# Gate, pool-output and attention-output projections with tokens on partitions, and four k-groups in place of five

## The chip, the core and the metric

The kernel runs on one core of a Trainium2 chip. The metric is the device time of one execution in microseconds (us), the median of repeated runs. The core has four engines that matter here: TensorE (PE in the profile, with its weight loads as PEld), VectorE (DVE), ScalarE (ACT) and GpSimd (POOL). SP is the queue that issues the loads.

## The reference

One decoder layer over 256 tokens and 2048 features, in float32, with an input projection 9280 columns wide:

```python
h = layer_norm(x) * (1.0 + scale) + shift          # shift, scale, gate = silu(c) @ w_ada + b_ada
q_lat, kv_lat, mla_gate, pool_in, pool_gate, gate_logits = split(h @ w_in)
y_mla = mla_mixer(q_lat, kv_lat, ...)               # 16 heads, causal
y_mla = (y_mla * silu(mla_gate)) @ w_mla_o
y_pool = pool_mixer(pool_in, w_pool_g, pool_scale)  # causal means over 2, 4, 8, 16 tokens, then w_pool_g
y_pool = (y_pool * silu(pool_gate)) @ w_pool_o
g_mla, g_pool = split(sigmoid(gate_logits + b_gates))
y = (g_mla * y_mla + g_pool * y_pool) @ w_out
out = layer_norm(alpha * x + (1.0 + gate) * y, ln_g, ln_b)
```

## The kernel before

Every float32 operand of a large product is split into two float32r tiles, `hi` and `lo`, whose sum is the operand. A product is then three matmuls: `mm3` (lines 95 to 98) multiplies high by high, high by low and low by high, with the weights standing still in the array (128 features) and all 256 tokens streaming. So the results of `w_in`, `w_pool_o` and `w_mla_o` have features on partitions. The last projection (`out_mm`, lines 922 to 928) is the other way round: 128 tokens stand still and 512 columns of weights stream.

Weights come in blocks of up to 1 MB into one of 5 raw tiles (`Raw`, `RAWB`), and are taken from there in parts of up to 1024 columns (`Job`): ScalarE writes `hi` (line 92), VectorE writes `lo` (line 93), into one of 4 pairs (`HB`). `execute` lets the loads and the splits run ahead of the matmuls as far as these tiles reach.

The work is a list of jobs, put in order by `weave`, which sets side work at given fractions of the main work:

1. The input projection goes over its 16 k-tiles in five groups (`KGROUPS`: 2, 3, 3, 4, 4 k-tiles). In each group all 72 feature tiles are done; `win_jobs` adds the group's sum to a tile in SBUF, by ScalarE in the first group (line 430) and by VectorE in the others (line 432). After the last group `post` applies silu or sigmoid.
2. Into each group but the last, the modulation of the next group's k-tiles is woven (`ada_jobs`): `w_ada` is multiplied by silu(c) and summed on VectorE (line 275), and `finish` sums over partitions on TensorE (line 300) and makes the next `hh` and `hl`. This is woven into the first 0.80 to 0.85 of a group (`WB`).
3. Into the last group go the norm of the latents, the rotary key, the pooling means and their mixing (`mix_jobs`).
4. Attention by pairs of heads, with the projections of the next pair and `pool_out` woven in. A head is done in four steps: `scores`, `normal` (scales the probabilities on VectorE), `transp` (three transposes on TensorE), `values` (features on partitions).
5. `mla_out`, which also merges the branches into `mh` and `ml`; then the output projection, the residual and the closing norm. The gate's modulation (`gate_jobs`) is woven into stages 4 and 5.

A scheduler sets each engine's final order from the kernel's text, so neighbouring jobs interleave.

Of the kernel before, what the change touches and what calls it, by code (L numbers as in the profile page):

```python
# [9 lines left out]
F32 = mybir.dt.float32  # L10
# [5 lines left out]
P = 128  # L16
# [28 lines left out]
ORD = ((0, 0), (1, 1), (2, 2), (3, 3))  # L45
GA = ((0, 0.1, 0.7),)
# [10 lines left out]
KGROUPS = ((0, 2), (2, 3), (5, 3), (8, 4), (12, 4))  # L57
# [3 lines left out]
def hybrid_layer(  # L61
# [38 lines left out]
    # A weight block is fetched whole into a raw tile and taken from it in parts;  # L100
    # a part becomes a pair of float32r tiles whose sum is the part exactly.
# [112 lines left out]

    c_sb = const.tile([P, KT], F32, name="c_sb")
# [44 lines left out]
    # adaLN modulation, in column blocks that follow the k-tiles of the input projection  # L260
# [129 lines left out]
    # input projection, transposed: features on partitions, tokens in the free dimension  # L390
    reg = {n: [] for n in ("qkv", "pi", "pg", "gp", "mg", "gm")}
# [8 lines left out]
    def post(name, f, src):  # L400
        dst = dest(name, f, src.shape[1])
        if name in ("mg", "pg"):
            A.activation(dst, src, AF.Silu)
        else:
            b = VB_G + (16 if name == "gp" else 0) + f
            for i in range(src.shape[1]):
                A.activation(dst[:, i, :], src[:, i, :], AF.Sigmoid, bias=vT[:, b + i:b + i + 1])

    def win_jobs(name, k0, nk, first, last, start=0):
        half = HALF // (nk * P)  # L410
        nft = 8 if name in ("qkv", "pi", "pg") else 16
        open_ps = {}

        def fn(wh, wl, f0):
            for fi in range(half):
# [10 lines left out]
                if f % 2 == 1:  # L426
                    dst = dest(name, f - 1, 2)
                    pv = ps.rearrange("p (a n) -> p a n", a=2)
                    if first:
                        A.copy(dst, pv)  # L430
                    else:
                        V.tensor_tensor(dst, pv, dst, op=ALU.add)
                    if last and name not in ("qkv", "pi"):
                        post(name, f - 1, dst)
# [12 lines left out]
    # the first features take the first two k-tiles one by one  # L447
# [20 lines left out]
    def proj_T(wv, nkt, col, xh, xl, done):  # L468
        banks = {}

        def fn(wh, wl, kc, b):
            if kc == 0:
                banks[b] = bank()
            for i in range(2):
                for k in range(4):
                    mm3(
                        banks[b][:, i * S:(i + 1) * S], wh[:, k, i * P:(i + 1) * P], wl[:, k, i * P:(i + 1) * P],
                        xh[kc][:, k, :], xl[kc][:, k, :], kc == 0 and k == 0 and i == 0,
                        kc == nkt // 4 - 1 and k == 3,
                    )  # L480
            if kc == nkt // 4 - 1:
                done(b, banks[b].rearrange("p (a n) -> p a n", a=2))

        jobs = []
        for kc in range(nkt // 4):
            jobs += block(
                wv[:, kc * 4:(kc + 1) * 4, col:col + 512], 4, 512,
                [lambda a, b, q=q, kc=kc: fn(a, b, kc, q) for q in range(2)], "c",
            )
        return jobs  # L490

    # rotary tables
# [50 lines left out]
    # the shared rotary key: the two parts of its weights stand side by side as columns, and their halves  # L543
    # of the product are summed; it is kept in both halves of the partitions
# [31 lines left out]
    # rms norm of the latents; the sum over features comes broadcast to all partitions  # L576
# [40 lines left out]
    # pooling mixer  # L617
# [40 lines left out]
    def mix_jobs():  # L658
        def fn(wh, wl, i):
            zp = ck(name="zp")  # L660
            for g in range(2):
                ps = bank()
                for o in range(2):
                    for k in range(2):
                        j = 2 * g + k
                        mm3(
                            ps[:, o * S:(o + 1) * S], wh[:, j, o * P:(o + 1) * P], wl[:, j, o * P:(o + 1) * P],
                            pl_h[i][:, j, :], pl_l[i][:, j, :], k == 0, k == 1,
                        )
                for o in range(2):  # L670
                    j = 2 * g + o
                    f = 4 * i + j
                    V.scalar_tensor_tensor(
                        zp[:, j, :], ps[:, o * S:(o + 1) * S], vT[:, VB_PS + f:VB_PS + f + 1],
                        reg["pg"][i][:, j, :], op0=ALU.mult, op1=ALU.mult,
                    )
            zp_h.append(ck(F32R, name="zp_h"))
            zp_l.append(ck(F32R, name="zp_l"))
            split(zp, zp_h[i], zp_l[i])
# [4 lines left out]
        )  # L684
# [3 lines left out]
    def pool_out(cb):  # L688
        def done(b, ps):
            dst = reg["gp"][cb][:, 2 * b:2 * b + 2, :]  # L690
            V.tensor_tensor(dst, ps, dst, op=ALU.mult)

        return proj_T(w_pool_o_v, 8, cb * 512, zp_h, zp_l, done)

    def gate_mla(cb):
        return proj_T(w_in_v, KT, OFF_G + cb * 512, hh, hl, lambda b, ps: post("gm", 4 * cb + 2 * b, ps))

    # latent attention
# [6 lines left out]
    def latent_jobs(p, cur):  # L705
# [10 lines left out]
        # a head's rotary query fills all partitions: one part in each half  # L716
# [52 lines left out]
    # The second tile of queries sees all keys. For the first, the two parts of its keys stand  # L769
    # side by side as columns, and their halves of the product are summed.  # L770
# [31 lines left out]
    def transp(i):  # L802
        sb, st = probs.pop(i)
# [5 lines left out]
        probs[i] = pT  # L809

    def values(i):
        pT = probs.pop(i)
        qt = i // 4
        if i % 4 == 0:
            z_h.append(ck(F32R, name="zh"))
            z_l.append(ck(F32R, name="zl"))
        if i % 2 == 0:
            ys[0] = bank()
        o = (i % 2) * S
        py, vn = ys[0], vals[qt]  # L820
        T.matmul(  # L821
            py[:, o:o + S], lhsT=vn[:, 0, i % 4, :], rhs=pT[:, :S], start=True, stop=False, skip_group_check=True,
        )
        T.matmul(
            py[:, o + P:o + S], lhsT=vn[:, 1, i % 4, :], rhs=pT[:, S:], start=False, stop=True, skip_group_check=True,
        )
        if i % 2 == 1:
            sl = slice(i % 4 - 1, i % 4 + 1)
            zf = wk(512, "zf").rearrange("p (a n) -> p a n", a=2)
            V.tensor_tensor(zf, py.rearrange("p (a n) -> p a n", a=2), reg["mg"][qt][:, sl, :], op=ALU.mult)  # L830
            split(zf, z_h[qt][:, sl, :], z_l[qt][:, sl, :])
# [38 lines left out]
    def mla_out(cb):  # L870
        def done(b, ps):
            if b == 0:
                mh.append(ck(F32R, name="mh"))
# [195 lines left out]
```

## Time and profile before

| | |
|---|---|
| runs | 816.19 us median of 3 (816.05, 816.19, 820.01) |
| profiled execution | span 817.3 us from its first to its last instruction; no other time of it is given |
| TensorE | 783.5 us busy (96%), 6149 matmuls |
| VectorE | 673.5 us busy (82%) |
| ScalarE | 426.2 us busy (52%) |
| loads | 192.6 MB on the SP queue, 237 GB/s over the span |

Busy time of TensorE is the union of its matmuls' spans, whose ends are modelled and overlap; how fast it works is read from the distance between starts.

### The profile page before, as it was taken

Reading aid. Unit: us, or ns where it says so; the run is one execution under the profiler, and the core shown is the slowest. Engines: PE = TensorE matmul, PEld = TensorE weight load, DVE = VectorE, ACT = ScalarE, POOL = GpSimd, SP = SyncE. Lnnn points to the kernel's source line nnn. Section 1 sums busy time; section 2 is a strip of 40 time slices with the busy share of each in tenths; the row PEclk is TensorE's granted clock in tenths of the full one; section 3 lists DMA queues with packets and bytes.
Section 4 is the critical chain, followed back from the end, with each engine's and each line's share of the span. In section 5 each row is a group of like instructions: output and inputs, shape, how many; then the busy total and the mean of one; then the engine's idle time right before and its main releaser. Section 6 shows DMA issues by size and latency. Waiting matters only on the chain.

```text
span 817.3 us, 15013 instructions
## 1 busy us (share of the span) xinstructions
PE 783.5 (96%) x6149; PEld 767.2 (94%) x6149; DVE 673.5 (82%) x1008; ACT 426.2 (52%) x609; POOL 7.6 (1%) x43
## 2 busy tenths in 40 slices
PE   2799999999999999999999999999999999999993
PEld 2699999999999999999999999999999999988883
DVE  6786889889979896788998878987775899878855
ACT  5577543433353333456686676666664444444521
POOL 1000000000000000000000000000000000000002
PEclk9799999999999999999999999999999999999998
DMA  9998688779979987553564555765444698899502
GB/s 279 333 378 292 231 270 287 252 254 305 314 265 329 319 289 238 166 174 116 201 206 145 186 189 189 245 196 194 156 156 155 217 313 292 281 392 355 210 1 103
DMA packets 106220, 193.57 MB, mean 237 GB/s; under 512 B 6356, under 2 KB 28068, under 8 KB 106152
## 3 DMA queue, kind: packets, MB, share of 16 engines
q1 hardware_dynamic: 106152, 192.62, 70.0%
q8 instruction: 48, 0.79, 0.4%
q14 instruction: 20, 0.16, 0.1%
HBM read 190.51 MB, written 2.10 MB: 236 GB/s over the span
## 4 chain that ended last, share of the span: by engine, by line
PE 94%; DMA 3%; DVE 2%; SPq 0%; ACT 0%; issue 0%; DVEq 0%
PE ps L96 25%; PE ps L98 25%; PE ps L97 25%; PE ps L927 4%; PE ps L926 4%; PE ps L928 4%; DMA raw<-in_w_in_dram 2%; PE ps L741 1%; PE ps L742 1%; PE ps L743 1%; DMA x<-in_x_dram 1%; PE ps L821 1%; PE ps L777 1%; PE ps L300 1%; PE ps L806 1%; PE ps L781 0%
## 5 line engine op out<-in xcount | busy, mean ns | idle before, releaser
L92 ACT ACTIVATE hi<-raw 128x1024 fp32r<-128x1024 f32 (+2 forms) x274 | 270.3, 987 | 315.9 <-PE ps L97 236.4
L93 DVE TENSOR_TENSOR lo<-raw,hi 128x1024 fp32r<-128x1024 f32 (+2 forms) x272 | 308.1, 1134 | 58.4 <-ACT hi L92 56.5
L96 PE MATMUL ps<-hh,hi 128*128 128x256 f32 x1152 | 326.2, 286 | 5.5 <-ACT hh L92 4.7
L97 PE MATMUL ps<-hl,hi 128*128 128x256 f32 x1152 | 327.2, 285 | 0.0
L98 PE MATMUL ps<-hh,lo 128*128 128x256 f32 x1152 | 325.5, 285 | 0.5 <-DVE lo L93 0.5
L96 PEld LDWEIGHTS ps<-hh,hi 128*128 128x128 f32 x1152 | 221.8, 193 | 6.2 <-ACT hh L92 5.0
L97 PEld LDWEIGHTS ps<-hl,hi 128*128 128x128 f32 x1152 | 223.0, 194 | 0.3 <-DVE hl L93 0.2
L98 PEld LDWEIGHTS ps<-hh,lo 128*128 128x128 f32 x1152 | 222.1, 194 | 0.7 <-DVE lo L93 0.7
L275 DVE SCALAR_TENSOR_TENSOR acc<-raw,s_c,acc 128x512 f32<-128x512 f32 (+3 forms) x148 | 125.3, 858 | 10.1 <-DMA raw<-in_w_ada_dram 9.3
L96 PE MATMUL ps<-zh,hi 128*128 128x256 f32 x256 | 72.4, 285 | 0.0
L98 PE MATMUL ps<-zh,lo 128*128 128x256 f32 x256 | 72.3, 283 | 0.0
L97 PE MATMUL ps<-zl,hi 128*128 128x256 f32 x256 | 72.3, 283 | 0.0
L98 PEld LDWEIGHTS ps<-zh,lo 128*128 128x128 f32 x256 | 49.1, 192 | 0.1
L97 PEld LDWEIGHTS ps<-zl,hi 128*128 128x128 f32 x256 | 49.1, 192 | 0.0
L96 PEld LDWEIGHTS ps<-zh,hi 128*128 128x128 f32 x256 | 48.9, 192 | 0.0
L96 PE MATMUL ps<-cn_h,hi 128*128 128x256 f32 x160 | 46.2, 289 | 0.0
L97 PE MATMUL ps<-cn_l,hi 128*128 128x256 f32 x160 | 45.3, 283 | 0.0
L98 PE MATMUL ps<-cn_h,lo 128*128 128x256 f32 x160 | 45.3, 283 | 0.0
L927 PE MATMUL ps<-lo,mh 128*128 128x512 f32 (+1 forms) x120 | 45.1, 376 | 0.0
L928 PE MATMUL ps<-hi,ml 128*128 128x512 f32 (+1 forms) x120 | 45.1, 375 | 0.0
L926 PE MATMUL ps<-hi,mh 128*128 128x512 f32 (+1 forms) x120 | 44.7, 376 | 0.0
L96 PE MATMUL ps<-zp_h,hi 128*128 128x256 f32 x128 | 36.4, 284 | 0.0
(203 smaller groups left out, 1068.8 us busy)
## 6 DMA issues: line engine op xcount, KB each, us to landing
raw<-in_w_in_dram SPq DMA_DIRECT2D x45, 1024.0 KB, 5.7
raw<-in_w_in_dram SPq DMA_DIRECT2D x36, 768.0 KB, 5.7
raw<-in_w_ada_dram SPq DMA_DIRECT2D x40, 512.0 KB, 5.6
raw<-in_w_ada_dram SPq DMA_DIRECT2D x16, 1024.0 KB, 5.0
raw<-in_w_mla_o_dram SPq DMA_DIRECT2D x16, 1024.0 KB, 5.4
raw<-in_w_out_dram SPq DMA_DIRECT2D x16, 1024.0 KB, 7.2
raw<-in_w_ada_dram SPq DMA_DIRECT2D x32, 384.0 KB, 5.2
raw<-in_w_kv_b_dram SPq DMA_DIRECT2D x8, 1024.0 KB, 5.3
```

The costliest lines, as they stand in the source:

```text
L92: A.activation(hi, src, AF.Copy)
L93: V.tensor_tensor(lo, src, hi.bitcast(F32), op=ALU.subtract)
L96: T.matmul(ps, lhsT=wh, rhs=xh, start=first, stop=False, skip_group_check=True)
L97: T.matmul(ps, lhsT=wh, rhs=xl, start=False, stop=False, skip_group_check=True)
L98: T.matmul(ps, lhsT=wl, rhs=xh, start=False, stop=last, skip_group_check=True)
L275: V.scalar_tensor_tensor(acc, src, s_c[:, t:t + 1], acc, op0=ALU.mult, op1=ALU.add)
L300: T.matmul(pa[:, j:j + 1], lhsT=acc[:, j * P:(j + 1) * P], rhs=ones[:, 0:1], start=i == 0, stop=i == len(accs) - 1,)
L741: T.matmul(o, lhsT=xh, rhs=w[0], start=k == 0, stop=False, skip_group_check=True)
L742: T.matmul(o, lhsT=xh, rhs=w[1], start=False, stop=False, skip_group_check=True)
L926: T.matmul(ps, lhsT=xh, rhs=wh[:, k, :], start=first and k == 0, stop=False)
L927: T.matmul(ps, lhsT=xh, rhs=wl[:, k, :], start=False, stop=False)
L928: T.matmul(ps, lhsT=xl, rhs=wh[:, k, :], start=False, stop=last and k == 1)
```

## The change

`w_in` for the four gates (`pg`, `gp`, `mg`, `gm`: 56 of the 72 feature tiles), `w_pool_o` and `w_mla_o` are now multiplied with tokens on partitions: `tok_jobs` lets 128 tokens stand still and 512 columns of weights stream (`mm3t`), with one PSUM bank for each half of the tokens. `qkv` and `pi` stay as they were. Gates and products then have tokens on partitions, so the bias of the sigmoid is no longer one value for each partition: it is loaded as a broadcast tile by POOL's queue and added on VectorE. Where the next product needs features on partitions, `turn` transposes a 256 x 512 block in eight transposes on TensorE, and the split reads PSUM: twice for the pool (`zp_turn`), four times after attention (`z_turn`), four times after `mla_out` (`m_turn`). In attention `normal` goes: the factor is applied with the gate in `values`, which is now three matmuls 128 wide in place of one 256 and one 128 wide.

The k-groups are 2, 4, 4, 6 and the modulation follows in pieces of 1, 1, 2, 2, 4, 2 and 4 k-tiles.

```diff
-KGROUPS = ((0, 2), (2, 3), (5, 3), (8, 4), (12, 4))
+KGROUPS = ((0, 2), (2, 4), (6, 4), (10, 6))
...
+    def mm3t(ps, xh, xl, wh, wl, first, last):
+        T.matmul(ps, lhsT=xh, rhs=wh, start=first, stop=False, skip_group_check=True)
+        T.matmul(ps, lhsT=xl, rhs=wh, start=False, stop=False, skip_group_check=True)
+        T.matmul(ps, lhsT=xh, rhs=wl, start=False, stop=last, skip_group_check=True)
...
+    def tok_jobs(wv, col, k0, nk, stat, done):
...
+            n = wh.shape[1]
+            for t in range(2):
+                for i in range(n):
+                    xh, xl = stat(k + i)
+                    ts = slice(t * P, (t + 1) * P)
+                    mm3t(banks[t], xh[:, ts], xl[:, ts], wh[:, i, :], wl[:, i, :], k + i == k0, k + i == k0 + nk - 1)
+            if k + n == k0 + nk:
+                done(banks)
...
+        for ka in range(k0, k0 + nk, UNIT // CB):
+            n = min(UNIT // CB, k0 + nk - ka)
+            cuts = list(range(0, n, 2)) + [n]
...
+    def turn(src, done):
+        for b in range(2):
+            pt = bank()
+            for a in range(2):
+                for t in range(2):
+                    T.transpose(
+                        pt[:, a * S + t * P:a * S + (t + 1) * P], src[:, t, (2 * b + a) * P:(2 * b + a + 1) * P], ident,
+                    )
+            done(b, pt.rearrange("p (a n) -> p a n", a=2))
...
+            for t in range(2):
+                if first:
+                    A.copy(dst[:, t, :], banks[t])
+                else:
+                    V.tensor_tensor(dst[:, t, :], banks[t], dst[:, t, :], op=ALU.add)
+            if last and name in ("mg", "pg"):
+                A.activation(dst, dst, AF.Silu)
+            elif last:
+                for t in range(2):
+                    V.tensor_tensor(dst[:, t, :], dst[:, t, :], biases.pop((name, cb, t)), op=ALU.add)
+                A.activation(dst, dst, AF.Sigmoid)
+
+        def bias():
+            b = wk(CB, "bias")
+            o = (D if name == "gp" else 0) + cb * CB
+            nc.gpsimd.dma_start(b, b_gates[0:1, o:o + CB].broadcast_to([P, CB]))
...
-    def normal(i):
...
-        for t, sl in tiles:
-            V.tensor_scalar(sb[:, sl], sb[:, sl], st[:, 2 + t:3 + t], None, op0=ALU.mult)
...
+        for t in range(2):
+            for j in range(t + 1):
+                T.matmul(
+                    py[:, a, t, :], lhsT=pT[:, (t + j) * P:(t + j + 1) * P], rhs=vn[:, j, i % 4, :],
+                    start=j == 0, stop=j == t, skip_group_check=True,
+                )
...
+            V.scalar_tensor_tensor(z, py[:, a, t, :], st[:, 2 + t:3 + t], z, op0=ALU.mult, op1=ALU.mult)
...
+        def done(banks):
+            m = tok["gm"][cb]
+            for t in range(2):
+                V.tensor_tensor(m[:, t, :], banks[t], m[:, t, :], op=ALU.mult)
+                V.tensor_tensor(m[:, t, :], m[:, t, :], tok["gp"][cb][:, t, :], op=ALU.add)
...
+    def m_turn(cb):
...
+        def done(b, ps):
+            sl = slice(2 * b, 2 * b + 2)
+            split(ps, mh[cb][:, sl, :], ml[cb][:, sl, :])
+
+        turn(tok["gm"][cb], done)
...
-    ADA = ((0, 1), (1, 1), (2, 3), (5, 3), (8, 4), (12, 4))
+    ADA = ((0, 1), (1, 1), (2, 2), (4, 2), (6, 4), (10, 2), (12, 4))
...
+    for cb in range(1, 4):
+        mo[cb][2:2] = todo(lambda cb=cb: m_turn(cb - 1))
...
+    oj[0][2:2] = todo(lambda: m_turn(3))
```

What stands on TensorE now is shown at two places, and SP's queue at a third. The numbers behind a name tell one buffer from another. First TensorE in a gate projection of the second k-group (`hh` and `hl` are the activations, `hi` and `lo` the weights). Before:

```order
L96 MATMUL ps_1385<-hh_246,hi_1299 128x256
L97 MATMUL ps_1385<-hl_247,hi_1299 128x256
L98 MATMUL ps_1385<-hh_246,lo_1300 128x256
...
L96 MATMUL ps_1385<-hh_937,hi_1299 128x256
L97 MATMUL ps_1385<-hl_938,hi_1299 128x256
L98 MATMUL ps_1385<-hh_937,lo_1300 128x256
```

and now:

```order
L104 MATMUL ps_1347<-hi_1298,hh_830 128x512
L105 MATMUL ps_1347<-hi_1298,hl_831 128x512
L106 MATMUL ps_1347<-lo_1299,hh_830 128x512
...
L104 MATMUL ps_1348<-hi_1298,hh_830 128x512
L105 MATMUL ps_1348<-hi_1298,hl_831 128x512
L106 MATMUL ps_1348<-lo_1299,hh_830 128x512
```

The streaming operand is named first: it was the activations, 256 wide, and is the weights, 512 wide. Twice as many columns go by for each matmul, and the number of matmuls halves.

Second, TensorE at the turn from the attention output to the output projection, in the changed kernel alone (`gm_869` is the last block of merged branches, `ps_6490` and `ps_6491` the banks of its two halves of tokens; L993 to L995 are the output projection). Before, no instruction stood between L98 and L926 here.

```order
L106 MATMUL ps_6491<-lo_6571,zh_6066 128x512
L993 MATMUL ps_6658<-hi_6588,mh_6168 128x512
...
L993 MATMUL ps_6658<-hi_6632,mh_6341 128x512
L994 MATMUL ps_6658<-lo_6633,mh_6341 128x512
L260 MATMUL ps_6705<-ident_82,gm_869 128x128
L260 MATMUL ps_6712<-ident_82,gm_869 128x128
L995 MATMUL ps_6658<-hi_6632,ml_6342 128x512
L260 MATMUL ps_6705<-ident_82,gm_869 128x128 x3
L260 MATMUL ps_6712<-ident_82,gm_869 128x128 x3
L993 MATMUL ps_6658<-hi_6632,mh_6341 128x512
```

Twenty-six matmuls of the next projection have been put between the last matmul of the block and its first transpose.

Third, SP's queue where the loads of the first k-group begin. Before:

```order
L109 DMA raw_221<-in_w_in_dram 128x2x1024
L109 DMA raw_231<-in_w_ada_dram 128x2x384 x2
L502 DMA pos_416<-in_positions_dram 128x256
L109 DMA raw_287<-in_w_in_dram 128x2x1024
L109 DMA raw_297<-in_w_ada_dram 128x2x384 x2
L109 DMA raw_304<-in_w_in_dram 128x2x1024
```

and now:

```order
L117 DMA raw_221<-in_w_in_dram 128x2x1024
L117 DMA raw_231<-in_w_ada_dram 128x4x256 x2
L117 DMA raw_287<-in_w_in_dram 128x2x512
L117 DMA raw_297<-in_w_ada_dram 128x4x256 x2
L117 DMA raw_304<-in_w_in_dram 128x2x512
L549 DMA pos_421<-in_positions_dram 128x256
L117 DMA raw_314<-in_w_in_dram 128x2x512
L117 DMA raw_321<-in_w_ada_dram 128x4x256 x2
```

A gate block of the first k-group fills half a raw tile (0.5 MB, two k-tiles of 512 columns) where it filled a whole one, and a block of the modulation has 1 MB where it had 0.79.

## Rows read from the trace of the kernel before

**Rows 1.** The page: span, and busy time of two engines.

```profile
span 817.3 us, 15013 instructions
...
PE 783.5 (96%) x6149; PEld 767.2 (94%) x6149; DVE 673.5 (82%) x1008; ACT 426.2 (52%) x609; POOL 7.6 (1%) x43
```

**Rows 2.** Stretches: length, then PE, PEld, DVE, ACT, POOL busy, PE clock, DMA.

```profile
161.00:240.00 79.00, 79.00 (x662) 79.00 (x662) 71.77 (x89) 33.79 (x42) 0.00 (x0) 1.00 0.87 292
...
450.00:640.00 190.00, 190.00 (x1570) 189.11 (x1569) 149.50 (x302) 123.08 (x235) 0.00 (x0) 1.00 0.56 184
640.00:716.00 76.00, 76.00 (x631) 75.81 (x631) 67.90 (x86) 33.36 (x38) 0.00 (x0) 1.00 0.85 288
716.00:793.00 77.00, 77.00 (x343) 63.76 (x342) 57.26 (x67) 33.00 (x33) 0.00 (x0) 1.00 0.68 250
```

**Rows 3.** The page: the chain that ended last, by engine.

```profile
PE 94%; DMA 3%; DVE 2%; SPq 0%; ACT 0%; issue 0%; DVEq 0%
```

**Rows 4.** Timeline of PE, 256 wide: first and last of 144 rows.

```profile
99.72 0.28 PE L96 MATMUL ps<-hh,hi 128*128 128x256 f32 x1
...
116.88 0.28 PE L98 MATMUL ps<-hh,lo 128*128 128x256 f32 x1
```

**Rows 5.** Timeline of PE, 512 wide: first and last of 108 rows.

```profile
719.67 0.39 PE L927 MATMUL ps<-lo,mh 128*128 128x512 f32 x1
...
743.93 0.39 PE L926 MATMUL ps<-hi,mh 128*128 128x512 f32 x1
```

**Rows 6.** Groups by shape: L96's three that change; L97, L98 have as many.

```profile
L96 PE MATMUL ps<-hh,hi 128*128 128x256 f32 x1152 | 326.2, 286 | 5.5 <-ACT hh L92 4.7 <-ACT hi L92 0.5 <-DVE mod_scale L307 0.3
...
L96 PE MATMUL ps<-zh,hi 128*128 128x256 f32 x256 | 72.4, 285 | 0.0
...
L96 PE MATMUL ps<-zp_h,hi 128*128 128x256 f32 x128 | 36.4, 284 | 0.0
```

**Rows 7.** Timeline of PE: transposes and values of one head in attention.

```profile
511.14 0.49 PE L806 MATMUL ps<-ident,sb 128*128 128x128 f32 x3
511.47 0.60 PE L821 MATMUL ps<-pT,vn 128*128 128x256 f32 x2
511.90 0.39 PE L824 MATMUL ps<-pT,vn 128*128 128x128 f32 x2
512.04 0.36 PE L96 MATMUL ps<-cn_h,hi 128*128 128x256 f32 x1
512.24 0.28 PE L97 MATMUL ps<-cn_l,hi 128*128 128x256 f32 x1
```

**Rows 8.** Timeline of DVE in the third and fourth k-groups.

```profile
186.34 0.68 DVE L432 TENSOR_TENSOR pi<-ps,pi 128x512 f32<-128x512 f32 x1
186.94 0.95 DVE L93 TENSOR_TENSOR lo<-raw,hi 128x768 fp32r<-128x768 f32 x1
187.81 1.28 DVE L275 SCALAR_TENSOR_TENSOR acc<-raw,s_c,acc 128x1024 f32<-128x1024 f32 x1
189.01 0.68 DVE L432 TENSOR_TENSOR pg<-ps,pg 128x512 f32<-128x512 f32 x1
...
262.15 1.22 DVE L93 TENSOR_TENSOR lo<-raw,hi 128x1024 fp32r<-128x1024 f32 x1
263.29 0.68 DVE L432 TENSOR_TENSOR pi<-ps,pi 128x512 f32<-128x512 f32 x1
```

**Rows 9.** Stretches of the start and of the first k-group, columns as in rows 2.

```profile
0.00:40.00 40.00, 19.08 (x104) 17.41 (x105) 28.64 (x72) 21.34 (x30) 2.60 (x39) 0.89 0.99 305
40.00:70.00 30.00, 30.00 (x248) 30.00 (x247) 24.40 (x24) 23.07 (x34) 0.00 (x0) 0.98 1.02 368
70.00:84.00 14.00, 14.00 (x119) 14.00 (x119) 6.34 (x8) 9.96 (x17) 0.00 (x0) 1.00 0.66 224
```

**Rows 10.** Timeline of PE: the modulation's finish in the first k-group.

```profile
80.03 1.40 PE L300 MATMUL ps<-ones,acc 128*128 128x1 f32 x12
```

**Rows 11.** Waits: who waited for whom; total, times, longest.

```profile
ACT hi L92 <- PE ps L97: 236.4, 171, 2.7
```

More of the change, by code (lines that the diff above doesn't have):

```diff
@@ L45 @@
 ORD = ((0, 0), (1, 1), (2, 2), (3, 3))
+CB = 512
 GA = ((0, 0.1, 0.7),)
@@ L398, in dest, with win_tok_jobs @@
         return reg[name][f // 4][:, f % 4:f % 4 + n, :]
[L400 to L407, printed above, removed]
+    def win_tok_jobs(name, cb, k0, nk, first, last):
+        def done(banks):
+            if first:
+                tok[name][cb] = ck(shape=(P, 2, CB), name=name)
+            dst = tok[name][cb]
+            for t in range(2):
+                if first:
+                    A.copy(dst[:, t, :], banks[t])
[12 more added lines that the diff above has]
+            for t in range(2):
+                biases[name, cb, t] = b
+        jobs = tok_jobs(w_in_v, OFFS[name] + cb * CB, k0, nk, lambda k: (hsl(hh, k), hsl(hl, k)), done)
+        if last and name in ("gp", "gm"):
+            jobs[1:1] = todo(bias)
+        return jobs
+    biases = {}
     def win_jobs(name, k0, nk, first, last, start=0):
         half = HALF // (nk * P)
-        nft = 8 if name in ("qkv", "pi", "pg") else 16
+        nft = 8
         open_ps = {}
@@ L466, in early_jobs @@
         )
[L468 to L490, printed above, removed]
     kpe = const.tile([P, 2, S], F32R, name="kpe")
@@ L808, in transp, with z_turn, done @@
         A.copy(pT, pt[:, :3 * P])
-        probs[i] = pT
+        probs[i] = pT, st
     def values(i):
-        pT = probs.pop(i)
-        qt = i // 4
[L814 to L831, printed above, removed]
+        pT, st = probs.pop(i)
+        qt, a = i // 4, i % 2
+        if a == 0:
+            ys[0] = bank()
+        py, vn = ys[0].rearrange("p (a t n) -> p a t n", a=2, t=2), vals[qt]
+        for t in range(2):
+            for j in range(t + 1):
+                T.matmul(
+                    py[:, a, t, :], lhsT=pT[:, (t + j) * P:(t + j + 1) * P], rhs=vn[:, j, i % 4, :],
+                    start=j == 0, stop=j == t, skip_group_check=True,
+                )
+        cs = slice((i % 4) * P, (i % 4 + 1) * P)
+        for t in range(2):
+            z = tok["mg"][qt][:, t, cs]
+            V.scalar_tensor_tensor(z, py[:, a, t, :], st[:, 2 + t:3 + t], z, op0=ALU.mult, op1=ALU.mult)
+    def z_turn(i):
+        if i % 4 != 3:
+            return
+        qt = i // 4
+        z_h.append(ck(F32R, name="zh"))
+        z_l.append(ck(F32R, name="zl"))
+        def done(b, ps):
+            sl = slice(2 * b, 2 * b + 2)
+            split(ps, z_h[qt][:, sl, :], z_l[qt][:, sl, :])
+        turn(tok["mg"][qt], done)
     g1 = []
@@ L1000, in hybrid_layer @@
     J += latent_jobs(0, pairs[0])
+    stages = ((scores, 0), (transp, 2), (values, 3), (z_turn, 5))
+    last = max(d for _, d in stages)
     att = []
@@ L1010, in hybrid_layer @@
         steps = []
-        for i in (2 * p, 2 * p + 1):
-            for f, d in ORD:
-                if i >= d:
-                    steps.append(Job(lambda f=(scores, normal, transp, values)[f], i=i - d: f(i)))
-        if p == H // 2 - 1:
-            for i in (H, H + 1, H + 2):
-                for f, d in ORD:
-                    if d and i - d < H and i >= H:
-                        steps.append(Job(lambda f=(scores, normal, transp, values)[f], i=i - d: f(i)))
+        for i in range(2 * p, 2 * p + 2 if p < H // 2 - 1 else H + last):
+            for f, d in stages:
+                if 0 <= i - d < H:
+                    steps.append(Job(lambda f=f, i=i - d: f(i)))
         att += weave(fill, (steps, 0.0, 1.0))
```

95 lines of the change are left out of this document (55 added, 40 removed).

## The prediction

> **What bounds the kernel now.** I read the page first: the span is 817.3 us and TensorE is busy 96% of it, VectorE 82% [rows 1]. Busy shares are averages, so I looked at stretches: from about 40 us to 793 us TensorE is busy in every microsecond of every stretch, at full clock (1.00) [rows 2]; VectorE comes next with 71.8 of 79 us in the third k-group and 67.9 of 76 in the attention output. The chain that ended last says the same from the other end: 94% of it is TensorE, 3% loads, 2% VectorE [rows 3]. ScalarE's largest wait is for TensorE to give back a split tile: 236 us in 171 waits [rows 11]. So the splits run ahead, and TensorE is never starved. The time after the start is then the sum of the distances between TensorE's starts, and a change is worth what it does to that sum, unless it makes TensorE wait.
>
> **The distance between starts.** 256 wide: 143 steps from 99.72 to 116.88 us [rows 4], 17.16/143 = 0.1200 us each. 512 wide: 107 steps from 719.67 to 743.93 us [rows 5], 24.26/107 = 0.2267 us. Two of the first cost 0.2400, so a matmul has 13.3 ns of its own beside its columns. In the 256-wide stages the weight loads fill the time too (PEld 79.0 of 79 us), in the 512-wide stage they do not (63.8 of 77) [rows 2].
>
> The Trainium skill (TensorE: Matmul & The Clock Gate, Back-to-back issue gap) puts that share at about 2.5 ns at full clock: 109.2 ns for 256 columns and 215.8 for 512. By it the change would save 4.8 us of matmuls and spend about 4.5 on transposes, so the time would stay at 816; the trace disagrees with its 0.1200 and 0.2267, and decides.
>
> **The change on TensorE.** Lines 96 to 98 have 1152, 256 and 128 matmuls each for `w_in`, `w_mla_o` and `w_pool_o` [rows 6]. Of `w_in`'s, 56 of 72 feature tiles change: 896. So 3 x (896 + 256 + 128) = 3840 matmuls of 256 columns become 1920 of 512.
> - Matmuls: 3840 x 0.1200 = 460.8 us become 1920 x 0.2267 = 435.3: minus 25.5 us.
> - Transposes: ten turns of eight are 80. Three in attention take 0.33 us (511.14 to 511.47) [rows 7], 0.11 each: plus 8.8 us. The bounds: 4.4 if a run of eight hides half of each (rival F), and 10.4 if each of some 20 runs pays 0.08 for the change, as L96 behind the values does (0.20 to L97 in place of 0.12).
> - Values: one head takes 0.65 us (511.47 to 512.24, less one 0.12) [rows 7], in two matmuls of float32 that show as two passes each. Three 128 wide are six passes; at a transpose's 0.11 that is 0.66: plus 0.2 us for 16 heads. If each head pays such a 0.08 once more, 1.5.
> - The mixing keeps 48 matmuls of 256 columns, the modulation's finish as many matmuls as before: 0.
>
> The sum is -25.5 + 8.8 + 0.2 = -16.5 us. Start (the first 40 us) and tail are unchanged: the first loads, the early blocks, the last projection and the closing norm stand as they did.
>
> **What has to stay hidden.** Steps of VectorE from [rows 8]: an addition of 512 from PSUM 0.60 us, `lo` of 768 0.87 and of 1024 1.14, a modulation step of 1024 1.20 (of 512 about 0.63, by the same ratio to a 512 addition).
> - Fewer groups: 36 pairs of feature tiles are added once less: 36 x 0.60 = 22 us off VectorE. The bias gives back 16 x 0.6 = 10; `normal`, the products with the gate and the splits of the turns about cancel. VectorE is not the bound, so this gains nothing by itself.
> - The fullest place is now the third k-group, with six k-tiles of modulation: `lo` 36 x 1.14 = 41, additions 36 x 0.60 = 22, modulation 16 x 0.63 + 16 x 1.20 = 29, in all 92 us under a TensorE time of 16 x 4 x 3 x 0.12 + 14 x 24 x 0.2267 = 99. In its woven part (0.85) it is 83 of 84 us. Before, the third group had 36 x 0.87 + 22 + 19 = 72 of 77, in the woven part 64 of 66, and TensorE did not wait [rows 2]. The cover is four split parts, 4 x 2.7 = 11 us.
> - Loads of the first k-group: four k-tiles of modulation where there were three, 2.1 MB more. At 368 GB/s in 40 to 70 us, then 224 to 84 us [rows 9], there is room for (368 - 224) x 14 us = 2.0 MB. In the new order 22.6 MB must land before the last modulation unit of the group; 305 x 40 us + 368 x 30 us = 23.2 MB had landed by 70 us. The finish of the modulation stood at 80.0 us [rows 10]; by the paces above 2.9 us less work stands ahead of it now, so 77. At 368 GB/s the last unit lands at 40 + 10.4/0.368 = 68 us and takes 2.5 on VectorE, so some 6 us are to spare. But a gate block there is half a raw tile, so five tiles hold less.
> - The bias loads are on POOL's queue, with nothing behind them but the closing norm. VectorE waits for each in order, and its next `lo` stands behind it; a bias is issued after the first of three parts, two parts (5.4 us) ahead, and the split cover of 11 us is behind that. The trace has no load of this kind: the price is 0 to a few us.
> - The turns: a transpose that waits holds up all of TensorE, which it never did for a merge. Behind the last matmul of a block the order puts other matmuls ahead of its last transposes: 8.4, 10.0, 9.1 and 6.3 us at the four `m_turn`s, 6.0 after the last head, 4.1 to 8.3 at the pool. VectorE needs two to four steps of 0.60 us (2.4), and by its row of instructions up to 2 x 0.63 of modulation and 1.14 of `lo` between them: 4.9. So each is covered if VectorE comes to it no more than 1 to 4 us late.
>
> I allow 1.4 us for small waits at the ten turns, 0.14 each. The profiled execution then has 817.3 - 16.5 + 1.4 = 802.2 us of span; its span is 1.1 us above the median of the runs, so the time is **801.0 us**.
>
> **The rivals.**
> A. The forecast, TensorE's sum with less than 8 us of new waits: 797 to 809. For it: TensorE waits nowhere now. Chance 0.76.
> B. VectorE or the loads fall behind in the first or third k-group. With VectorE's durations in place of its steps (`lo` 1.22, addition 0.68, modulation 1.28 [rows 8], 0.72 for 512) the woven part needs 90 of 84 us: 6 late, if the cover of split parts is not there. If half-filled tiles hold the first group's loads to 224 GB/s, the last unit lands at 40 + 10.4/0.224 = 86 us and is summed at 89, 12 late. So 807 to 813. Against: the third group of before was as full, and the loads ran at 368 with five tiles too. Chance 0.09.
> C. A pace of 0.24 for 512 columns in these stages, where VectorE and the loads are busier: the matmuls save nothing, and the turns cost 9.0: 825. It breaks even at 0.2353, and is slower by 0.5% from 0.2375. Against: in the stretch of [rows 2] from 716 us loads and splits run too, and no step there is longer. Chance 0.03.
> D. TensorE waits at the turns, the other side: it needs 2.1 us at each of ten, on top of a cover of 4 to 10, to lose the 20.6 us that lie between the forecast's sum (799.7) and 820.3. If VectorE comes 6.3 us late (one modulation unit of four steps, a `lo`, four merging steps), covers of 4 to 6 us fall short by 4 us in all: 804. Only a VectorE that is 7 to 8 us late at all of them gives 820 or more; it is busy 67.9 of 76 us where the `m_turn`s are [rows 2]. Chance 0.04.
> E. The 13.3 ns belong to the last projection alone, and here a pair saves 4.7 ns or less (9.0 us over 1920): no change, 816. Against: the 256-wide step is 0.1200 in the stage that changes, and columns alone would have to take the 0.235 that remain, which they do not in [rows 5]. Chance 0.03.
> F. Better than 797: if runs of eight transposes hide half of each behind the next, 4.4 us come off: 797 without any wait. Chance 0.05.
>
> **How the numbers follow.** The likeliest is A, 801.0. Its range and the half of B below 810 hold 0.81: 797 to 810. What tells from no change is 0.5%, 4.1 us. Faster: A, F and most of B, 0.88. Same: the rest of B, E and a part of D, 0.06. Slower: C and most of D, 0.06.
>
> **What would show it.** Steps of 0.2267 us on lines 104 to 106 in all three uses; 80 transposes at 0.11; TensorE busy in every microsecond from 40 us to the end; the finish of the first group's modulation near 77 us; the last matmul some 15 us earlier. I am wrong if the step is longer (C, E), if TensorE shows idle time ahead of line 260 (D), or ahead of 104 or 350 in the first and third groups (B).

## The result, and the profile after

The changed kernel takes **804.23 us** (median of 4 runs, 803.0 to 804.53) beside 816.28 for the kernel before (4 runs): a ratio of 0.984, 95% interval 0.982 to 0.986. A second set of runs, `after_again` below, gave 803.81 (ratio 0.983, 0.982 to 0.984). So the gain is 12 us; 15 were predicted, and 804.2 lies inside the range.

The page of the changed kernel answers to [rows 1, 3]:

```profile
span 802.7 us, 11355 instructions
...
PE 767.0 (96%) x4341; PEld 673.1 (84%) x4341; DVE 660.0 (82%) x987; ACT 419.6 (52%) x572; POOL 12.1 (2%) x51
...
PE 90%; DMA 6%; DVE 2%; ACT 1%; SPq 0%; issue 0%; DVEq 0%
```

TensorE is still the chain, but loads have gone from 3% of it to 6%. Its weight loads no longer fill the time (84%, was 94%). In stretches, columns as in [rows 2] (those of the first k-group answer to [rows 9]):

```profile
40.00:70.00 30.00, 28.61 (x139) 23.52 (x138) 25.75 (x34) 21.80 (x35) 0.69 (x1) 1.00 1.05 351
70.00:84.00 14.00, 13.76 (x64) 11.03 (x63) 11.95 (x14) 11.40 (x18) 0.00 (x0) 1.00 1.00 348
...
157.00:256.00 99.00, 99.00 (x540) 86.34 (x539) 90.63 (x107) 41.66 (x45) 0.54 (x1) 1.00 0.87 295
...
640.00:716.00 76.00, 76.00 (x352) 62.91 (x351) 64.53 (x81) 35.02 (x39) 0.00 (x0) 1.00 0.83 287
```

From 84 us on TensorE is busy throughout at full clock, through the third k-group and the `m_turn`s too. Only the first k-group has holes, where before it had none. The timeline of TensorE answers to [rows 5] (first and last of 58 rows) and [rows 7] (two transposes of a turn):

```profile
646.08 0.38 PE L260 MATMUL ps<-ident,gm 128*128 128x128 f32 x2
646.22 0.48 PE L104 MATMUL ps<-hi,zh 128*128 128x512 f32 x1
646.54 0.40 PE L105 MATMUL ps<-hi,zl 128*128 128x512 f32 x1
...
664.03 0.40 PE L104 MATMUL ps<-hi,zh 128*128 128x512 f32 x1
...
676.96 0.39 PE L104 MATMUL ps<-hi,zh 128*128 128x512 f32 x1
```

57 steps in 12.93 us are 0.2268 each, the pace predicted, with loads at 287 GB/s beside them. From the first transpose to the second matmul behind it are 0.46 us: less 0.2267 for the one matmul, two transposes cost 0.23, 0.12 each. Where the change of kind shortens one step (0.14 for two transposes) it lengthens the next (0.32), so a run pays next to nothing extra. Taken in this way, all 19 runs of transposes in the trace sum to 8.8 us for 80, 0.110 each.

To see where the other 3 us are, I added up all distances between TensorE's starts and compared each with the step of its kind (0.2267, 0.1200, 0.11, and 0.216 for the float32 passes of 256 columns in the old `values`). In the changed kernel the steps sum to 758.7 us; in the kernel before, profiled a second time, to 775.2: minus 16.5, as predicted. From 42 us on, the distances exceed the steps by 4.7 us in the changed kernel, by 0.4 before. 2.8 of the 4.7 are in one place, 60 to 80 us. There, all engines (columns: start, duration, engine, line, operation, what the engine waited for; other rows left out):

```profile
62.30 3.11 DVE L325 SCALAR_TENSOR_TENSOR acc<-raw,s_c,acc 128x512 f32<-128x512 f32 x4 [1.39 <-DMA raw<-in_w_ada_dram]
...
63.57 1.06 ACT L93 ACTIVATE hi<-raw 128x1024 fp32r<-128x1024 f32 x1 [0.66 <-DMA raw<-in_w_in_dram]
...
65.33 1.22 DVE L94 TENSOR_TENSOR lo<-raw,hi 128x1024 fp32r<-128x1024 f32 x1
...
66.60 0.50 PE L106 MATMUL ps<-lo,hh 128*128 128x512 f32 x1 [0.67 <-DVE lo L94]
...
67.83 0.59 ACT L458 COPY mg<-ps 128x512 f32<-128x512 f32 x1 [2.21 <-PE ps L106]
...
68.31 1.06 ACT L93 ACTIVATE hi<-raw 128x1024 fp32r<-128x1024 f32 x1
...
69.43 0.50 PE L104 MATMUL ps<-hi,hh 128*128 128x512 f32 x1 [0.72 <-ACT hi L93]
...
70.86 0.50 PE L104 MATMUL ps<-hi,hh 128*128 128x512 f32 x1 [0.24 <-ACT hi L93]
```

TensorE waits for split parts that were made just before, because VectorE (62.30) and ScalarE (63.57) had waited for raw tiles to land. The split at 68.31 shows no wait of its own, since it stands behind a copy that waited for TensorE (67.83), but it too was late by its load: the blocks that ScalarE splits at 63.57, 68.31 and 69.74 were issued at 54.18, 59.57 and 60.93 us and landed at 63.54, 67.87 and 69.24, some 8 to 9 us later. That points to a lack of loads; VectorE is nearly full there too (6.79 of 7 us from 65 us on), and the experiments tell the two apart.

### The profile page after: what moved, and what is told of

Its sections match the earlier page's. It is cut to its first block, busy times and chain, and to the rows that moved or that the text cites. A ratio compares the mean times of both kernels' runs of the same rounds, so it can differ in the third digit from the quotient of the medians.

```text
span 802.7 us, 11355 instructions
## 1 busy us (share of the span) xinstructions
PE 767.0 (96%) x4341; PEld 673.1 (84%) x4341; DVE 660.0 (82%) x987; ACT 419.6 (52%) x572; POOL 12.1 (2%) x51
## 4 chain that ended last, share of the span: by engine, by line
PE 90%; DMA 6%; DVE 2%; ACT 1%; SPq 0%; issue 0%; DVEq 0%
PE ps L106 17%; PE ps L104 17%; PE ps L105 17%; PE ps L98 6%; PE ps L97 6%; PE ps L99 6%; DMA raw<-in_w_in_dram 4%; PE ps L993 4%; PE ps L995 4%; PE ps L994 4%; PE ps L870 1%; PE ps L260 1%; DMA raw<-in_w_ada_dram 1%; PE ps L797 1%; PE ps L796 1%; PE ps L798 1%
## 5 line engine op out<-in xcount | busy, mean ns | idle before, releaser
L104 PE MATMUL ps<-hi,hh 128*128 128x512 f32 x448 | 175.3, 391 | 1.0 <-ACT hi L93 1.0
L105 PE MATMUL ps<-hi,hl 128*128 128x512 f32 x448 | 174.4, 389 | 0.0
L106 PE MATMUL ps<-lo,hh 128*128 128x512 f32 x448 | 167.5, 390 | 0.7 <-DVE lo L94 0.7
L325 DVE SCALAR_TENSOR_TENSOR acc<-raw,s_c,acc 128x512 f32<-128x512 f32 (+2 forms) x163 | 128.5, 799 | 12.0 <-DMA raw<-in_w_ada_dram 10.2
L97 PE MATMUL ps<-hh,hi 128*128 128x256 f32 x256 | 71.8, 287 | 4.7 <-ACT hh L93 4.4
L98 PE MATMUL ps<-hl,hi 128*128 128x256 f32 x256 | 72.8, 286 | 0.3 <-DVE hl L94 0.3
L99 PE MATMUL ps<-hh,lo 128*128 128x256 f32 x256 | 72.5, 286 | 0.5 <-DVE lo L94 0.5
L97 PEld LDWEIGHTS ps<-hh,hi 128*128 128x128 f32 x256 | 48.7, 193 | 5.2 <-ACT hh L93 4.7
L98 PEld LDWEIGHTS ps<-hl,hi 128*128 128x128 f32 x256 | 49.7, 194 | 0.8 <-DVE hl L94 0.6
L99 PEld LDWEIGHTS ps<-hh,lo 128*128 128x128 f32 x256 | 49.6, 194 | 0.7 <-DVE lo L94 0.7
L97 PE MATMUL ps<-cn_h,hi 128*128 128x256 f32 x160 | 46.0, 288 | 0.0
L98 PE MATMUL ps<-cn_l,hi 128*128 128x256 f32 x160 | 45.2, 283 | 0.0
L995 PE MATMUL ps<-hi,ml 128*128 128x512 f32 (+1 forms) x120 | 45.1, 376 | 0.0
```

The lines of the kernel that those rows point to most:

```text
L97: T.matmul(ps, lhsT=wh, rhs=xh, start=first, stop=False, skip_group_check=True)
L98: T.matmul(ps, lhsT=wh, rhs=xl, start=False, stop=False, skip_group_check=True)
L99: T.matmul(ps, lhsT=wl, rhs=xh, start=False, stop=last, skip_group_check=True)
L104: T.matmul(ps, lhsT=xh, rhs=wh, start=first, stop=False, skip_group_check=True)
L105: T.matmul(ps, lhsT=xl, rhs=wh, start=False, stop=False, skip_group_check=True)
L106: T.matmul(ps, lhsT=xh, rhs=wl, start=False, stop=last, skip_group_check=True)
```

## The experiments

All are timed beside the kernel before, but for the first.

**Before again.** No edit; one profile.

> The kernel before, unchanged, profiled once more. Theory (the profiled execution of before was a slow-starting one: 10.2 us of it at half clock before 42 us of span, against 3.4 us in the changed kernel): a new execution is at 815.5 to 816.5 us with a span some 1.8 us shorter (814 to 815), and less of its start is at half clock. Rival (the half-clock stretches belong to the kernel before, and the change shortened them): again about 10 us at half clock, time 816 to 818.

816.42 us with a span of 814.5: the time is 1.9 us above the span. The 817.3 of [rows 1] was then an execution of some 819, not one near the median. Its last matmul started at 804.14 us; in the second profile:

```profile
span 814.5 us, 15013 instructions
```

```profile
801.33 0.28 PE L928 MATMUL ps<-hi,ml 128*128 128x256 f32 x1
```

The 2.8 us lie before 42 us (mean clock in 20 to 40 us 0.77 in the first profile, 0.91 in the second and in the changed kernel). So the change did not shorten the half-clock stretches; the theory holds, by two profiles of one kernel.

**The k-groups alone**, on the old projections:

```diff
-KGROUPS = ((0, 2), (2, 3), (5, 3), (8, 4), (12, 4))
+KGROUPS = ((0, 2), (2, 4), (6, 4), (10, 6))
```

(and `ADA` as in the change)

> Only the k-groups and the modulation groups of the change, on the old projections with features on partitions. Theory (TensorE's steps set the time; fewer merges only lighten VectorE, which is not the bound): TensorE has the same 256-wide steps, so 815 to 818, ratio 0.999 to 1.002; a little of it may be a wait in the first group, which now has a k-tile more of modulation to load. Rival (fewer merges are worth something, since VectorE is 82% busy): 36 merges x 0.6 us = up to 22 us less on VectorE would show as 3 us or more of time, 813 or less.

817.12 us, ratio 0.9999 (0.999 to 1.0007): nothing. VectorE's busy time went from 673.5 us to 659.3:

```profile
PE 783.1 (96%) x6149; PEld 766.7 (94%) x6149; DVE 659.3 (81%) x991; ACT 427.0 (52%) x610; POOL 7.6 (1%) x43
```

That is 14 us less and not the 22 of the additions alone, for the modulation comes in smaller pieces, with more instructions. It is worth nothing where VectorE is not the bound. In the first group there are already two gaps of some 0.4 us at 66 to 67 us, 0.9 in all by the distances between starts.

**Tokens alone**: the changed kernel with the two lines on groups put back.

> Only the tokens on partitions, with the old k-groups 2, 3, 3, 4, 4 and the old modulation groups. Theory (the 2 to 3 us that TensorE waits at 65 to 71 us of the changed kernel come from the modulation that the first group has to load and sum, four k-tiles in place of three): that wait is gone, TensorE's steps are the same, so 801.5 to 803, 1 to 3 us under the changed kernel's 804.2. Rival (the fewer groups are needed so that VectorE keeps up with 512-wide steps): 22 us more merges on VectorE, TensorE waits in the later groups, 806 or more.

819.93 us, ratio 1.0036 (1.002 to 1.005): **slower than before**, 15.7 us above the changed kernel. The theory was right about the first group (no gap at 60 to 80 us) and wrong about the whole. The rival is right; of the later groups that it named it is the last one. Stretches:

```profile
380.00:400.00 20.00, 20.00 (x95) 16.76 (x94) 20.00 (x33) 13.19 (x14) 0.76 (x1) 1.00 0.58 192
400.00:410.00 10.00, 9.72 (x53) 8.10 (x52) 10.00 (x16) 7.03 (x9) 0.00 (x0) 1.00 0.47 169
410.00:420.00 10.00, 8.58 (x38) 6.81 (x37) 10.00 (x18) 8.27 (x11) 0.00 (x0) 1.00 0.64 210
420.00:430.00 10.00, 10.00 (x46) 8.24 (x45) 10.00 (x15) 6.53 (x8) 1.08 (x2) 1.00 0.73 237
430.00:440.00 10.00, 10.00 (x57) 8.75 (x56) 10.00 (x18) 5.20 (x5) 1.08 (x2) 1.00 0.70 233
440.00:452.00 12.00, 3.46 (x16) 2.53 (x15) 10.04 (x18) 7.41 (x7) 0.00 (x0) 0.84 0.55 178
```

VectorE is busy in every microsecond from 380 to 440, and TensorE then waits for the pooled tile:

```profile
PE ps L104 <- ACT pl_h L93: 8.5, 1, 8.5
```

The last group holds the norm of the latents, the pooling, the last merges and the 16 bias additions, whatever its length in k-tiles. Four k-tiles of 512-wide steps take some 99 us of TensorE (16 x 4 x 3 x 0.12 + 14 x 24 x 0.2267); six take 149. At 400 to 460 us TensorE loses 12.6 us. It also starts some 4.6 us later: by 42 us it has done 12.1 us of steps, the changed kernel 16.7. The granted clock from 20 to 42 us is 0.69 in this profile and 0.92 in the changed kernel's. The kernel before had 0.77 and 0.91 from 20 to 40 us in its two profiles, so how much of this start belongs to the old groups is not shown.

**Is VectorE the cause there?** Two edits. First, the bias additions to POOL:

```diff
-V.tensor_tensor(dst[:, t, :], dst[:, t, :], biases.pop((name, cb, t)), op=ALU.add)
+G.tensor_tensor(dst[:, t, :], dst[:, t, :], biases.pop((name, cb, t)), op=ALU.add)
```

> Tokens on partitions with the old k-groups (the kernel that took 819.9 us), and the 16 additions of the gates' bias moved from VectorE to POOL: 16 x 0.68 = 10.9 us less on VectorE in the last k-group, the same results. Theory (that kernel lost its gain because the last group, four k-tiles of 512-wide steps, is too short for VectorE's norms, pooling, merges and bias; TensorE then waited 8.5 us for the pooled tile and 2 us for split tiles): VectorE has 10 us to spare again, most of the 12.6 us of waits at 400 to 452 us go, 805 to 811. Rival (the pooled tile is late by its place in the order, or by ScalarE): the wait for the pooled tile stays at 7 us or more, 817 to 820.

822.23 us, ratio 1.006 (1.005 to 1.007): no gain, both theories' numbers missed. The wait for the pooled tile's `hi` fell to 2.1 us, but one of 2.6 for its `lo` came behind it, and waits for split tiles came too (2.7 at 400 us, 2.2 at 446). VectorE was as full as before (20 of 20 us from 380 to 400, 400 to 420 and 420 to 440), since its instructions were stretched while POOL's ran (see the last section). So it tells nothing on the cause. Second, the additions and their loads left out, so that the result lacks the bias:

```diff
-                for t in range(2):
-                    V.tensor_tensor(dst[:, t, :], dst[:, t, :], biases.pop((name, cb, t)), op=ALU.add)
...
-            jobs[1:1] = todo(bias)
```

> Tokens on partitions with the old k-groups (819.9 us), without the 16 additions of the gates' bias and their loads; it leaves out the bias. VectorE has 16 x 0.68 = 10.9 us less in the last k-group, and nothing is given to POOL, whose additions had stretched VectorE's own instructions (a modulation step of 0.74 us to 2.89, one of 0.19 to 1.27). Theory (VectorE is the bound of the last group there, and TensorE's 12.6 us of waits at 400 to 452 us are its excess): at least 9 of the 12.6 us go, VectorE has idle time in 400 to 450 us, 808 to 811; the 4 to 5 us that this kernel is behind the changed one by 42 us stay. Rival (the wait is the place of the pooled tile in the order): the waits stay at 8 us or more, 815 to 820.

810.79 us (807.93 to 811.99), ratio 0.992 (0.991 to 0.994). Stretches:

```profile
400.00:420.00 20.00, 20.00 (x96) 16.82 (x96) 20.00 (x34) 16.11 (x20) 0.00 (x0) 1.00 0.66 211
420.00:440.00 20.00, 18.08 (x94) 15.16 (x93) 16.72 (x25) 11.85 (x12) 0.00 (x0) 1.00 0.57 181
440.00:452.00 12.00, 11.51 (x70) 9.95 (x68) 8.22 (x13) 6.21 (x10) 0.00 (x0) 1.00 0.53 158
```

10.9 us of VectorE's work taken out of the last group took 9.1 us off the time, and 3.0 of the 12.6 us of waits remain (the profiled execution, 807.93, is the fastest of the six). The loads that went with the additions are no rival: in `tokens_alone` VectorE was busy there and did not wait for them. So VectorE is the bound of that group when it has four k-tiles.

**The gaps of the first group.** Half of the modulation's loads for k-tiles 2 to 5 left out (so its sum is not the right one), with the same instructions:

```diff
+            j = i % (per // 2) if half else i
-            src = raw[:, i * w:(i + 1) * w]
+            src = raw[:, j * w:(j + 1) * w]
```

(and `pieces` fetches half of each unit)

> The changed kernel with half of the modulation weights of k-tiles 2 to 5 left out of the loads (each unit reads the half that it has twice), so 4.2 MB less in the first k-group and the same instructions on VectorE and TensorE; it leaves out that part of the computation. Theory L (the wait at 65 to 71 us comes from loads: the DMA engines are at a share of 1.02 to 1.06 there, and ScalarE and VectorE wait for raw tiles): no TensorE wait over 0.3 us in 60 to 75 us, time 801 to 802.5, 2 to 3 us under the changed kernel. Rival V (VectorE is late, because a modulation unit of four steps, 3.1 us, stands ahead of each lo): the gaps of 0.4 to 0.9 us ahead of lines 104 and 106 stay, time 803.5 to 804.5.

803.42 us, ratio 0.983 (0.982 to 0.985). The gaps at 65 to 71 us are gone in its profile: from 60 to 70 us TensorE is busy 10.00 of 10 us.

```profile
60.00:70.00 10.00, 10.00 (x46) 8.29 (x45) 6.54 (x11) 6.71 (x11) 0.00 (x0) 1.00 0.83 259
70.00:80.00 10.00, 7.98 (x36) 6.38 (x35) 9.29 (x11) 7.12 (x12) 0.00 (x0) 0.98 0.85 281
```

VectorE's steps are as many as before, so the gaps come from the loads (theory L). But the time fell by only 0.4 to 0.8 us, not by 2 to 3: in the profiled execution (808.35 us, the slowest of the six) TensorE then waits 2.0 us for the modulation's sum at 77 us, and from 81 us some twelve steps run at half clock (mean 0.68 in 80 to 90 us). Why the sum is late there is not settled; the loads ran at 0.8 of the DMA's time, with raw tiles half full. Whether the five faster executions wait there too is not known, nor, then, that all of the gaps' 2.8 us could be won.

**The same loads, spread thinner**:

```diff
-WB = (0.85, 0.85, 0.85, 0.8)
+WB = (0.95, 0.85, 0.85, 0.8)
```

> The changed kernel with the modulation units of the first k-group woven up to 0.95 of it in place of 0.85: the same work, with the modulation's loads spread thinner over the weight blocks. Theory L (TensorE's 2.1 us of gaps at 65 to 71 us are the weight blocks' loads, which stand behind too many modulation loads at a saturated DMA rate): some 0.7 MB less stands ahead of the blocks there, 2 us at 345 GB/s, so the gaps shrink to under 1 us; 802 to 803.5, if the finish of the modulation, which then stands some 5 us later, does not become a wait of its own at the start of the next group, at 82 to 86 us (then 804 to 806).

804.91 us, ratio 0.985 (0.982 to 0.987). The gaps did not shrink, they moved to 73 to 77 us (2.05 us), and the next group's first tile came late by 1.1 us, at 87 us. I read it as the same loads, which have to land before the group ends; no run separates that from VectorE's work on them. TensorE's waits from 42 to 110 us (who waited for whom; total, times, longest):

```profile
PE ps L106 <- DVE lo L94: 1.2, 2, 0.7
PE ps L98 <- DVE hl L94: 1.1, 1, 1.1
PE ps L104 <- ACT hi L93: 0.4, 1, 0.4
```

**A k-tile less of modulation in the first group**:

```diff
-KGROUPS = ((0, 2), (2, 4), (6, 4), (10, 6))
+KGROUPS = ((0, 2), (2, 3), (5, 4), (9, 7))
```

(and `ADA` in pieces of 1, 1, 1, 2, 4, 1, 2, 4)

> The changed kernel with k-groups 2, 3, 4, 7: a k-tile less of modulation (2.1 MB) in the first group, four in the second, seven in the third, and a last group that is longer still. Theory (the gaps at 65 to 71 us go with the fourth k-tile of modulation, and VectorE keeps up elsewhere as long as the last group is long): no gaps there, 801 to 803. Rival (VectorE falls behind in the third group: 0.85 x (41 + 22) + 35 = 88.6 us of its steps for 84 us of TensorE's, less a cover of 11 us of split parts): TensorE waits ahead of lines 104 to 106 or 350 in the third group, 804 to 809. From tokens alone (819.9 us, where VectorE was busy in every microsecond of the last 60 us of its last group and TensorE waited 8.5 us for the pooled tile) the last group is expected to show no wait.

815.55 us, ratio 0.998 (0.997 to 1.000). The gaps of the first group are gone, and the last group has none; but the third loses 11.8 us:

```profile
PE ps L350 <- DVE acc L325: 9.1, 1, 9.1
```

```profile
200.00:220.00 20.00, 10.90 (x42) 8.89 (x41) 19.29 (x24) 4.01 (x7) 0.00 (x0) 0.74 0.95 334
```

The rival came true, above its 809. By its working VectorE is 4.6 us short over the woven part, and the cover was to hide that. Why it does not is argued only: the small modulation pieces stand first, and TensorE needs the sum of one of them at 204 us, while VectorE, busy 16.8 of 20 us from 180 to 200, is full only from 200 on. The clock takes its part: the mean is 0.74 over the 20 us, and 0.50 from 210 to 218. With some of that group's `lo` halves made on POOL:

```diff
+            if gi == 2:
+                for jb in main[3::6]:
+                    jb.eng = G
```

> K-groups 2, 3, 4, 7 (815.6 us), with the lo half of every sixth split part of the third group made by POOL in place of VectorE: some 6 x 1.2 = 7 us less on VectorE there. Theory (TensorE's 9.3 us wait ahead of line 350 at 204 us is VectorE's excess in that group, and the cold clock behind it is a consequence): both go, and since the first group has no gaps with three k-tiles of modulation, 801 to 804, as fast as the changed kernel or 2 us under it. Rival (POOL's parts come late, some 2.5 us each, and TensorE waits for them; or POOL's work slows VectorE's): 806 or more.

811.13 us, ratio 0.992 (0.991 to 0.993). The wait falls from 9.1 to 5.3 us and no more; the numbers lie with the rival, and the trace shows its second form, POOL holding up VectorE (last section).

**The price of a transpose.** Each transposed twice:

```diff
-                for t in range(2):
+                for t in (0, 1, 0, 1):
                     T.transpose(
```

> The changed kernel with each of the 80 transposes of the turns done twice, the second over the first. Theory (0.11 us each, nothing hidden): 80 x 0.11 = 8.8 us longer, 812 to 814. Rival F (half of each lies behind the next in a run of eight, now sixteen): 4.4 us, 808 to 809. Rival D (VectorE's next step after a turn was on TensorE's path): over 10 us, with idle time on TensorE ahead of line 260 or behind it.

812.29 us, 8.1 above 804.23.

```profile
652.74 1.69 PE L260 MATMUL ps<-ident,gm 128*128 128x128 f32 x14
654.19 0.47 PE L106 MATMUL ps<-lo,zh 128*128 128x512 f32 x1
654.50 0.39 PE L104 MATMUL ps<-hi,zh 128*128 128x512 f32 x1
```

From the first of these 14 transposes to the second matmul behind them are 1.76 us: less 0.2267, 0.11 each. The steps sum to 8.8 us more, with no idle time at any turn; the rest is a start that was 0.35 us ahead and gaps in the first group of 2.4 in place of 2.8. F's hidden half is out.

**The price of a matmul.** Each 512-wide matmul of `mm3t` as two of 256:

```diff
-        T.matmul(ps, lhsT=xh, rhs=wh, start=first, stop=False, skip_group_check=True)
...
+            m = ps.shape[1] // 2
+            for h in range(2):
+                hs = slice(h * m, h * m + m)
+                T.matmul(
+                    ps[:, hs], lhsT=x_, rhs=w_[:, hs], start=first and n == 0 and h == 0, stop=last and n == 2,
```

> The changed kernel with each 512-wide matmul of lines 104 to 106 issued as two of 256 with the same stationary tile, so 1920 more matmuls (some 1850 after the mixing's, which become 128 wide) and the same columns, transposes and merges. Theory (a matmul has 13.3 ns of its own beside its columns, wherever it stands): 1920 x 13.3 ns = 25.5 us longer, 829 to 831. Rival E (an own cost of 2.5 to 4.7 ns): 4.8 to 9 us longer, 809 to 813. A third way, that a matmul of 256 is held by its weight load (0.12 us each in the profile of before), would also give 0.12 a step: it shows as a weight load busy all of the time, and is not told from the first here.

832.11 us (829.53 to 834.43), ratio 1.018 (1.015 to 1.021): 27.9 above 804.23. The steps sum to 30.3 more: 25.5 for 1920 matmuls, as expected, and 4.9 that I had left out: the mixing's 48 became 96, 128 wide, and these take 0.111 us (2.23 us for 20 steps, between the rows below), not the 0.067 that columns and 13.3 ns would make. Against that, the gaps of the first group went from 2.8 to 0.2 us: a slower TensorE asks for no more than the loads bring.

```profile
447.12 0.38 PE L108 MATMUL ps<-hi,pl_l 128*128 128x128 f32 x2
...
449.35 0.39 PE L108 MATMUL ps<-lo,pl_h 128*128 128x128 f32 x2
```

Rival E is out. The expectation's third way is not: the weight loads fill the time again (781.0 of 827.8 us, 94%), so whether a step of 0.1200 is held by its columns or by its weight load stays open. The price of the change is the same by either.

**After again.** No edit.

> The changed kernel once more, beside the two others on one chip. Theory: 803 to 805 us, TensorE's gaps at 65 to 71 us again 2 to 3 us in all, and the time from its last start to the end 13 to 14 us.

803.81 us (803.56 to 803.90), with gaps of 2.5 us at 60 to 80 us. The last matmul starts 14.1 us before the end of the span, as in the first profile; in both profiles of the kernel before it is 13.2.

## Why the prediction was nearly right

- **Matmuls** (minus 25.5 us): right. Steps of 0.2268 on lines 104 to 106, and `halves` gives the 25.5 back.
- **Transposes** (plus 8.8): right, by `turns_twice` and the 0.110 each in the changed kernel. **Values** (plus 0.2, 1.5 at most): right within the sum, minus 16.5 in all. **Bias loads** (0 to a few us): 0, VectorE waits for none of them.
- **Loads of the first k-group** (0; "some 6 us are to spare"): the largest miss, which the sum put at nothing. The group's modulation is indeed finished at 76.6 us, as forecast (77):

```profile
76.59 0.95 PE L350 MATMUL ps<-ones,acc 128*128 128x1 f32 x8
```

  But I had looked only at the last modulation unit. The weight blocks share the same loads, and TensorE now takes them faster; at a DMA share of 1.05 and 351 GB/s (368 in [rows 9]) they come late in the middle of the group, at 65 to 71 us. That is 2.8 us, rival B's place at a quarter of its price. `tokens_alone` and `groups_2347` show that it goes with the fourth k-tile of modulation, `half_ada_loads` that it goes with the bytes, VectorE's work being the same. `halves` shows that TensorE's pace matters as well: with the same loads and 256-wide steps 0.2 us of gaps are left. The half-filled raw tiles that the forecast named are in `tokens_alone` and `groups_2347` too, without a gap, so by themselves they are not it.
- **Small waits at the turns** (plus 1.4): wrong. TensorE waits at none of them, in the changed kernel and in `turns_twice`, and rival D is out. Outside the first k-group the excess is 1.9 us against 0.4 before, but it lies in small amounts over the matmuls of the whole kernel; that 1.5 is near 1.4 is chance.
- **Fewer groups** ("gains nothing by itself"): right to the word (`groups_alone`, 0.9999), but misleading. With tokens on partitions they are worth 15.7 us, most of it because without them VectorE is the bound of the last group (12.6 us of waits there). I had looked for the fullest place in the third group, where TensorE indeed does not wait (VectorE 90.6 of 99 us), and not at what the last one would be with the old groups. The two halves of the change do not add.
- **Tail unchanged** (0): 0.9 us longer in both profiles. VectorE's and ScalarE's instructions there take the same; the end of the last store is later. What delays it was not found.
- **The base** ("its span is 1.1 us above the median"): the time is 1.9 us above the span, so the profiled execution of before was some 3 us slow, all in its start. This took nothing from the forecast: from the second profile, 814.5 - 16.5 + 1.4 + 1.9 gives 801.3.

The account of the spans: 814.5 to 802.7 is minus 11.8 = -16.5 (steps) + 4.3 (excess after 42 us, 2.7 of it in the first k-group) - 0.5 (start) + 0.9 (tail). So the forecast was near because its large terms were right; its allowance of 1.4 us stood for waits that did not come, and covered a third of others that did. No complete version tried beats the changed kernel by a measurable amount.

## What to carry to other kernels

Where one engine is busy all the time, a sum of its steps can price a change to within a microsecond, as it did here for the steps themselves; what was missed is in the stages where another engine or the loads become the bound, and each stage needs its own count of bytes against time at every point, not only at its end. When a change makes the bound engine faster, look for the shortest stage with a fixed load on the second engine: here that stage decided between 1.6% faster and 0.4% slower. A rearrangement that is worth nothing alone can be what lets another one pay.

## What the runs showed of the hardware

**POOL and VectorE hold each other up.** In `g2347_pool_lo` a modulation step of VectorE that takes 0.75 us elsewhere took 2.89; it had started 0.1 us behind an instruction of POOL and ended 0.5 us after it. VectorE, then POOL:

```profile
194.46 1.22 DVE L94 TENSOR_TENSOR lo<-raw,hi 128x1024 fp32r<-128x1024 f32 x1 [2.04 <-ACT hi L93]
195.60 2.89 DVE L325 SCALAR_TENSOR_TENSOR acc<-raw,s_c,acc 128x512 f32<-128x512 f32 x1
198.41 0.68 DVE L460 TENSOR_TENSOR pg<-ps,pg 128x512 f32<-128x512 f32 x1
```

```profile
195.51 2.44 POOL L94 TENSOR_TENSOR lo<-raw,hi 128x1024 fp32r<-128x1024 f32 x1 [15.08 <-ACT hi L93]
```

In `tokens_pool_bias` an instruction over 32 elements took 1.27 us in place of 0.18:

```profile
446.15 1.27 DVE L687 TENSOR_TENSOR pl<-win,rcount 128x32 f32<-128x32 f32 x1
```

POOL is held up as well: its additions of 512 there take from 1.27 to 2.30 us. The Trainium skill (SBUF — State Buffer, Who interferes with whom) says that a VectorE instruction with two inputs in SBUF contends with a GpSimd instruction that reads SBUF, and that whichever starts second blocks. Both stretched instructions have two tensors in SBUF as inputs and started behind POOL's, so the traces agree. In neither run did the work moved to POOL lower VectorE's busy time: 680.8 us beside 677.1 of `tokens_alone`, 663.9 beside 661.1 of `groups_2347`. The second run was faster all the same, by 4.4 us.

**A float32r matmul of 128 columns takes 0.111 us**, of 256 0.1200, of 512 0.2267 (`halves`): 128 columns cost nearly what 256 do. Whether the weight load or the stream sets the 0.111 is not told apart.

**A long wait cost more than itself.** TensorE waited 9.1 us in `groups_2347`, from 204.7 us on; from 210 to 218 us the granted clock was 0.50, half of full speed, also for the steps behind the wait, and the group lost 11.8 us in all. Behind the 2.0 us wait of `half_ada_loads` some twelve steps ran at half clock; the gaps of under 1 us at 65 to 71 us of the changed kernel left it at 1.00.
